# Low parts of the state space mixer's input weights made during the first feed-forward layer and kept in DRAM

## The chip, the cores and the metric

The kernel runs on one core of one Trainium2 chip. The metric is the device time of one execution in microseconds (us); lower is better. The core has TensorE (PE in the rows, with its weight loads as PEld), VectorE (DVE), ScalarE (ACT), GpSimd (POOL) and SyncE (SP). SP and POOL do little but issue DMAs here. Each engine runs its own instructions strictly in order and waits on semaphores for the others.

## The reference

The reference is a chain of two blocks of two layers each. The change concerns the second block alone: a gated linear attention mixer (GLA), a feed-forward layer, a state space mixer (SSD), and a second feed-forward layer. The feed-forward layer and the input side of the mixer, cut to what matters:

```
def sq_relu_mlp(h, w1, w2):                    # D = 1024, w1: D x 4D, w2: 4D x D
    return jnp.square(jax.nn.relu(h @ w1)) @ w2

def ssd_mixer(uc, ul, w_in, conv_w, conv_b, dt_bias, a_log, d_skip, norm_g, w_out, need_ctx):
    def run(h, s_init, need_y):                # h: 256 context or 256 latent tokens
        z, xbc, dt = jnp.split(h @ w_in, [SSD_DI, SSD_DI + SSD_CONV_DIM], axis=-1)
        xbc = jax.nn.silu(dwconv(xbc, conv_w, conv_b))
        xs, bm, cm = jnp.split(xbc, [SSD_DI, SSD_DI + SSD_GN], axis=-1)
        dt = jax.nn.softplus(dt + dt_bias)
        ... chunked scan over 64-token chunks in 8 groups of 4 heads, both directions ...
        return rms_norm_2(y * jax.nn.silu(z), norm_g) @ w_out, (s_f, s_b)
```

All data are fp32. `w_in` of the mixer has 1024 rows; its columns are z (2048), x (2048), B (1024), C (1024) and dt (64).

## The kernel before, in words

A product with weights in fp32 is made of three products of a shorter format: an operand is split into a high part, its cast, and a low part, what the cast left over. For each column block and each of the eight 128-row steps of the contraction (k-steps below) TensorE adds high weight times high input (L1135), high weight times low input (L1136) and low weight times high input (L1137). Inputs are split once. Weights are split each time they are loaded: `wparts` (L1083) loads a stretch with SP, lets ScalarE cast the high piece (L1100, tile `whi`) and lets VectorE subtract it from the loaded weight (L1101, tile `wlo`). `dense_pool(size, bufs)` sets how many columns a piece has and how many pieces can stand ready: 1024 and 4 in the feed-forward layers, 512 and 4 in the mixer. `dense_t` gives transposed outputs, `dense_n` (L1141, products L1155 to L1157) outputs by token rows.

The first feed-forward layer (`ffn(0)`) works on 512 tokens, context and latents. The SSD mixer (`ssd`) first normalizes and modulates its input (`mod_t`), makes dt and its running sums, and then goes over 8 groups. `ssd_in(g)` makes a group's inputs one group ahead: a product "both" of 384 columns (256 of x, 128 of B) for 512 tokens, 72 matmuls of 512 columns, and a product "latents" of 384 columns (128 of C, 256 of z) for 256 tokens, 72 matmuls of 256 columns. Each is followed by a convolution on VectorE (tile `cacc`). `ssd_group(g)` does the scan of the group before: copies of transposed x on ScalarE (`xn`), decays (`dec`, 16 exponents' inputs and 4 exponents), the row `cB` of 2048 columns (ScalarE, then VectorE), and small matmuls (`py`, `tp`). A group's weights come as 5 and 3 k-steps in two DMAs each.

The order on each engine is set at build time by a scheduler that works from a program's dependences, its own estimates of times and priorities: the two split instructions carry a higher priority than what is written around them (`high_priority(offset=300)`). On the chip the orders are fixed. Work that is to run beside other work is written as a generator; `tick` runs it one piece further.

Of the kernel before, what the change touches and what calls it, by code (L numbers as in the profile page):

```python
# [19 lines left out]
P = 128  # L20
# [17 lines left out]
class Kern:  # L38
    def __init__(self, tc, A, ctx):
        self.tc = tc  # L40
        self.nc = tc.nc
        self.A = A
        self.ctx = ctx
        self.cp = ctx.enter_context(tc.tile_pool(name="cp", bufs=1))
        self.cp0 = self.cp
        self.mods, self.beside = {}, None
        self.xp = ctx.enter_context(tc.tile_pool(name="xp", bufs=1))
# [6 lines left out]
        self.wown, self.wlen = None, 2048  # L54
        self.uid = 0
        self.consts()
# [1024 lines left out]
    def wparts(self, wap, k0, kn, cols):  # L1081
# [11 lines left out]
        for k1 in range(0, kn, ks):  # L1093
            hi = self.dp.tile([P, size], F32R, tag="whi", bufs=bufs, name=self.name("whi"))
            lo = self.dp.tile([P, size], F32R, tag="wlo", bufs=bufs, name=self.name("wlo"))
            kk = min(ks, kn - k1)
# [8 lines left out]
    def wbuf(self):  # L1105
# [3 lines left out]
        return self.wp.tile([P, self.wlen], F32, tag="w", bufs=self.wbufs, name=self.name("w"))  # L1109

    def wall(self, wap, nkd, cols):
        n = sum(c[1] for c in cols)
# [3 lines left out]

    def dense_t(self, xh, xl, wap, nkd, cols, emit, n=512, role="mm", parts=1):

# [6 lines left out]
        kw = dict(skip_group_check=True)  # L1125
        ws = self.wall(wap, nkd, cols)
        if parts > 1:
            ws = list(ws)
        for i in range(parts):
            t = slice(i * n // parts, (i + 1) * n // parts)  # L1130
            for k, wh, wl in ws:
                for b in range(nb):
# [3 lines left out]
                    nc.tensor.matmul(a, wh[:, cs], xl[:, k, t], start=False, stop=False, **kw)  # L1136
                    nc.tensor.matmul(a, wl[:, cs], xh[:, k, t], start=False, stop=k == nkd - 1, **kw)  # L1137
        for b in range(nb):
            emit(b, acc[b // pb][:, b % pb])

    def dense_n(self, xs, wap, nkd, cols, emit, mt, role="mm", row0=0, by_tile=False):  # L1141
# [17 lines left out]
        if by_tile:  # L1159
            ws = list(ws)  # L1160
            for m in range(mt):
                for w in ws:
                    step(m, *w)
                emit(m, acc[m][:, 0])
            return
        for w in ws:
            for m in range(mt):
                step(m, *w)
        for m in range(mt):
            emit(m, acc[m // pb][:, m % pb])  # L1170
# [636 lines left out]
    def ssd(self, X, gr, mods, spill):  # L1807
# [4 lines left out]
        self.roles.update(mm=[0, 1, 2, 3, 4], tp=[5, 6], py=[7])  # L1812
        with self.dense_pool(512, 4), self.tc.tile_pool(name=self.name("ssd"), bufs=1, reuse_waits="tile") as gp:
            xh, xl = self.slot(2, [P, KD, 512], F32R), self.slot(3, [P, KD, 512], F32R)
# [30 lines left out]
            self.norm_z(X, 0, *self.factors(st, 0, 2))  # L1845
        return X, gr

    def ssd_in(self, g, xh, xl, W, gp):
# [18 lines left out]

        self.dense_t(xh, xl, W, KD, [(2048 + 256 * g, 256), (4096 + 128 * g, 128)], put)
        self.dense_t(xh[:, :, S:], xl[:, :, S:], W, KD, [(5120 + 128 * g, 128), (256 * g, 256)], put_l, S)
        return xT, bT, cT, zs  # L1870
# [102 lines left out]
    def block2(self, x, mods, out):  # L1973
        X, gr, ctx = self.gla(x)
        self.gk.close()
        gr = self.ffn(0, X, mods[0], (1, 0), 2, 3, gr, ctx=ctx)
        X, gr = self.ssd(X, gr, mods[1], self.drp.tile([S, D], F32, name="x_ssd"))
# [55 lines left out]
```

## Time and profile before

| what | value |
|---|---|
| median of 3 runs | 2223.16 us (2219.62 to 2271.85) |
| the profiled execution's own time | 2227.16 us |
| its span in the profile | 2225.4 us |
| mean granted TensorE clock of that span | 0.962 of full speed |
| TensorE, VectorE, ScalarE busy | 92%, 63%, 40% of the span |
| GpSimd | 3%, 142 instructions |
| DMA | 464.60 MB moved, mean 209 GB/s |

The profile is of one execution on the one core. The busy shares are means over stages with different limits, so the stages are read one by one. By their instructions' lines they lie, from the span's start, at about 1245 to 1300 us (the end of the GLA mixer and the normalization behind it), 1300 to 1642 us (first feed-forward layer), 1642 to 1720 us (the mixer's input and its first products), 1720 to 1950 us (its groups), 1950 to 2003 us (last group and output product). The second feed-forward layer follows.

### The profile page before, as it was taken

Reading aid. Unit: us, or ns where it says so; the run is one execution under the profiler, and the core shown is the slowest. Engines: PE = TensorE matmul, PEld = TensorE weight load, DVE = VectorE, ACT = ScalarE, POOL = GpSimd, SP = SyncE. Lnnn points to the kernel's source line nnn. Section 1 sums busy time; section 2 is a strip of 40 time slices with the busy share of each in tenths; the row PEclk is TensorE's granted clock in tenths of the full one; section 3 lists DMA queues with packets and bytes.
Section 4 is the critical chain, followed back from the end, with each engine's and each line's share of the span. In section 5 each row is a group of like instructions: output and inputs, shape, how many; then the busy total and the mean of one; then the engine's idle time right before and its main releaser. Section 6 shows DMA issues by size and latency. Waiting matters only on the chain. (4 is left out here: it accounts for less than half of the span.)

```text
span 2225.4 us, 34842 instructions
## 1 busy us (share of the span) xinstructions
PE 2053.6 (92%) x13545; PEld 1584.1 (71%) x13545; DVE 1403.1 (63%) x3139; ACT 889.3 (40%) x1788; POOL 62.7 (3%) x142
## 2 busy tenths in 40 slices
PE   8999999896999999988799899999988999997997
PEld 7889655542787855543577598888877888877896
DVE  6864543545776553544786765444476999987666
ACT  5442233211454232221564432322335676755443
POOL 1000000000000000000000000000000000000001
PEclk9997999998999999999999999999998999998998
DMA  8656699888563899898655543223223343445552
GB/s 269 242 189 221 241 329 387 320 320 314 198 242 115 316 326 358 335 362 332 222 211 199 201 141 114 95 95 95 81 70 119 105 134 122 128 168 180 186 193 76
DMA packets 224962, 464.60 MB, mean 209 GB/s; under 512 B 32221, under 2 KB 111741, under 8 KB 217881
## 3 DMA queue, kind: packets, MB, share of 16 engines
q1 hardware_dynamic: 217080, 439.34, 55.8%
q0 software_dynamic: 7712, 22.99, 3.0%
q8 instruction: 108, 1.77, 0.3%
q14 instruction: 62, 0.50, 0.1%
HBM read 457.93 MB, written 4.36 MB: 208 GB/s over the span
## 5 line engine op out<-in xcount | busy, mean ns | idle before, releaser
L1101 DVE TENSOR_TENSOR wlo<-w,whi 128x512 fp32r<-128x512 f32 (+4 forms) x528 | 402.8, 773 | 289.2 <-ACT whi L1100 286.3
L1100 ACT CAST whi<-w 128x512 fp32r<-128x512 f32 (+4 forms) x528 | 358.3, 690 | 546.6 <-PE mm L1136 180.5
L1156 PE MATMUL mm<-wlo,xh 128*128 128x256 f32 (+1 forms) x544 | 159.5, 294 | 0.3 <-DVE wlo L1101 0.2
L1155 PE MATMUL mm<-whi,xh 128*128 128x256 f32 (+1 forms) x544 | 158.9, 294 | 1.0 <-ACT whi L1100 1.0
L1157 PE MATMUL mm<-whi,xl 128*128 128x256 f32 (+1 forms) x544 | 158.1, 292 | 0.0
L1156 PE MATMUL acc<-wlo,hh 128*128 128x512 f32 x384 | 148.6, 389 | 0.0
L1155 PE MATMUL acc<-whi,hh 128*128 128x512 f32 x384 | 147.7, 389 | 0.0
L1157 PE MATMUL acc<-whi,hl 128*128 128x512 f32 x384 | 146.0, 389 | 0.0
L1135 PE MATMUL mm<-s__2932_15020,whi 128*128 128x256 f32 (+1 forms) x384 | 131.0, 346 | 8.2 <-ACT etot L1786 3.9
L1136 PE MATMUL mm<-s__2933_15021,whi 128*128 128x256 f32 (+1 forms) x384 | 129.4, 342 | 0.0
L1137 PE MATMUL mm<-s__2932_15020,wlo 128*128 128x512 f32 (+1 forms) x384 | 118.8, 348 | 3.3 <-DVE wlo L1101 3.3
L1156 PEld LDWEIGHTS mm<-wlo,xh 128*128 128x128 f32 x544 | 105.8, 195 | 11.1 <-DVE isc L407 2.4
L1136 PE MATMUL mm<-s__2108_10494,whi 128*128 128x512 f32 (+1 forms) x320 | 110.3, 348 | 0.5 <-DVE s__2108_10494 L92 0.5
L1155 PEld LDWEIGHTS mm<-whi,xh 128*128 128x128 f32 x544 | 105.7, 195 | 6.3 <-issue 2.7
L1137 PE MATMUL mm<-s__2107_10493,wlo 128*128 128x512 f32 (+1 forms) x320 | 109.1, 350 | 0.9 <-DVE wlo L1101 0.9
L1135 PE MATMUL mm<-s__2107_10493,whi 128*128 128x512 f32 (+1 forms) x320 | 108.3, 349 | 1.1 <-ACT whi L1100 1.1
L1157 PEld LDWEIGHTS mm<-whi,xl 128*128 128x128 f32 x544 | 105.7, 195 | 0.8 <-issue 0.7
L818 PE MATMUL gu<-wx,xg 128*32 128x256 f32 x1024 | 94.2, 390 | 1.7 <-DMA wx<-in_expert_w_up_dram 1.6
L1135 PEld LDWEIGHTS mm<-s__2932_15020,whi 128*128 128x128 f32 x384 | 73.7, 192 | 17.4 <-ACT whi L1100 4.2
L1802 DVE SCALAR_TENSOR_TENSOR cacc<-mm,cvw,cacc 128x508 f32<-128x508 f32 (+3 forms) x128 | 82.2, 672 | 4.3 <-ACT cacc L1798 4.1
L1157 PEld LDWEIGHTS acc<-whi,hl 128*128 128x128 f32 x384 | 72.1, 188 | 15.0
L1156 PEld LDWEIGHTS acc<-wlo,hh 128*128 128x128 f32 x384 | 72.1, 188 | 14.8
(697 smaller groups left out, 4675.8 us busy)
## 6 DMA issues: line engine op xcount, KB each, us to landing
w<-in_ffn_w_dram SPq DMA_DIRECT2D x64, 1024.0 KB, 5.2
wx<-in_expert_w_down_dram SPq DMA_DIRECT2D x38, 1024.0 KB, 10.6
wx<-in_expert_w_up_dram SPq DMA_DIRECT2D x34, 1024.0 KB, 9.2
adaw<-in_ada_w_dram SPq DMA_DIRECT2D x32, 1024.0 KB, 6.6
wx<-in_expert_w_gate_dram SPq DMA_DIRECT2D x32, 1024.0 KB, 6.4
w<-in_expert_w_down_dram SPq DMA_DIRECT2D x28, 1024.0 KB, 11.8
w<-in_expert_w_gate_dram SPq DMA_DIRECT2D x26, 1024.0 KB, 9.9
w<-in_w_in_dram SPq DMA_DIRECT2D x24, 1024.0 KB, 8.8
```

The costliest lines, as they stand in the source:

```text
L818: nc.tensor.matmul(gu[j * CAP:(j + 1) * CAP, c * EH:(c + 1) * EH], xg[:, k, s:s + CAP], w(c, j, k), start=k == 0 and c == 0, stop=k == KD - 1,
L1100: nc.scalar.copy(hv, v[:, k1:k1 + kk])
L1101: nc.vector.tensor_sub(lv, v[:, k1:k1 + kk], hv.bitcast(F32))
L1135: nc.tensor.matmul(a, wh[:, cs], xh[:, k, t], start=k == 0 and b % pb == 0 and i == 0, stop=False, **kw)
L1136: nc.tensor.matmul(a, wh[:, cs], xl[:, k, t], start=False, stop=False, **kw)
L1137: nc.tensor.matmul(a, wl[:, cs], xh[:, k, t], start=False, stop=k == nkd - 1, **kw)
L1155: self.nc.tensor.matmul(a, h[:, sl], wh, start=k == 0 and m % pb == 0, stop=False, **kw)
L1156: self.nc.tensor.matmul(a, h[:, sl], wl, start=False, stop=False, **kw)
L1157: self.nc.tensor.matmul(a, o[:, sl], wh, start=False, stop=k == nkd - 1, **kw)
L1802: nc.vector.scalar_tensor_tensor(acc[:, :, t0:t1], a[:, :, t0 + o:t1 + o], w(t), acc[:, :, t0:t1], op0=OP.mult, op1=OP.add)
```

## The change

During `ffn(0)` a generator `presplit` runs beside the layer, moved on by `step`, which `dense_t` and `dense_n` now call. It has 48 items, one for each 512-column block (12) and each pair of k-steps (4). An item loads 512 KB of `ssd_w_in` with a DMA from POOL into `raw` (two buffers), casts two halves of 128x512 on ScalarE into `hi` (one buffer), subtracts them on VectorE into one half of a ring `parts`, and writes the 512 KB of low parts to DRAM (`lows`) with another DMA from POOL. Its tiles lie in space that GLA's constants had.

In the mixer `ssd_in` takes its weights from `wlows`: high pieces are loaded and cast as before, low pieces come from `lows`, two k-steps at a time, by two DMAs from SP into a `wlo` tile of 768 columns with four buffers. High pieces have three buffers instead of four. The splits of dt's weights and of the output product stay as they were.

```diff
+    def step(self):
+        if self.inner:
+            self.inner += 1
+            if self.inner % 5 in (1, 3):
+                self.tick()
...
+    def wlows(self, wap, nkd, cols, low):
...
+                nc.sync.dma_start(v[:, :, o:o + cn], wap[k0 * P:(k0 + kn) * P, c0:c0 + cn].rearrange("(k p) n -> p k n", p=P))
...
+            for k in range(kn):
+                if (k0 + k) % 2 == 0:
+                    lo = low(k0 + k, 2)
+                hi = self.dp.tile([P, 512], F32R, tag="whi", bufs=self.pieces[1], name=self.name("whi"))[:, :n]
+                with self.tc.high_priority(offset=300):
+                    nc.scalar.copy(hi, v[:, k])
+                yield k0 + k, hi, lo[:, (k0 + k) % 2]
...
-        with self.dense_pool(512, 4), self.tc.tile_pool(name=self.name("ssd"), bufs=1, reuse_waits="tile") as gp:
+        with self.dense_pool(512, 3), self.tc.tile_pool(name=self.name("ssd"), bufs=1, reuse_waits="tile") as gp:
+            self.wlow = 768
...
+    def presplit(self, W, pool, ring):
...
+        todo = [(c, k) for c in (4, 8, 10, 0, 5, 1, 6, 9, 11, 2, 7, 3) for k in range(0, KD, 2)]
...
+                t = raws[n] = pool.tile([P, 2, 512], F32, tag="raw", bufs=2, name=self.name("raw"))
+                nc.gpsimd.dma_start(t, W[k * P:(k + 2) * P, c * 512:c * 512 + 512].rearrange("(k p) n -> p k n", p=P))
...
+        for n, (c, k) in enumerate(todo):
+            load(n + 1)
...
+            for j in range(2):
+                hi = pool.tile([P, 512], F32R, tag="hi", bufs=1, name=self.name("hi"))
+                nc.scalar.copy(hi, raw[:, j])
...
+                nc.vector.tensor_sub(lo[:, :, j], by_g(raw[:, j]), by_g(hi.bitcast(F32)))
+            nc.gpsimd.dma_start(d[:, :, k:k + 2], lo.bitcast(F32))
+            yield
...
+        self.dense_t(xh, xl, W, KD, both, put, ws=parts(both))
+        self.dense_t(xh[:, :, S:], xl[:, :, S:], W, KD, latents, put_l, S, ws=parts(latents))
...
+            self.beside, self.inner = self.presplit(self.A["ssd_w_in_2"][0], pre, ring), 1
+            gr = self.ffn(0, X, mods[0], (1, 0), 2, 3, gr, ctx=ctx)
+            self.tick(100)
```

Three places show how the engines' orders change. The numbers at names are buffers; lines of the changed program are some 10 to 80 higher than before. First VectorE at the start of the mixer, where dt is made (`dt_t`) while the first group's products run. Before:

```order
L1754 RECIPROCAL dt_t_15157<-dt_t_15157 128x256
L1101 TENSOR_TENSOR wlo_15392<-w_15362,whi_15391 128x384
L1755 TENSOR_TENSOR dt_t_15157<-dt_t_15157,dt_t_15156 128x256
L1101 TENSOR_TENSOR wlo_15405<-w_15362,whi_15404 128x384
L1756 TENSOR_TENSOR dt_t_15156<-dt_t_15157 128x256
L1757 TENSOR_SCALAR dt_t_15158<-dt_t_15156 128x256
L1101 TENSOR_TENSOR wlo_15418<-w_15362,whi_15417 128x384
L1759 SCALAR_TENSOR_TENSOR dt_t_15158<-dt_t_15158,dt_t_15156 128x256
L1101 TENSOR_TENSOR wlo_15434<-w_15430,whi_15433 128x384
```

The same place in the changed program:

```order
L1786 RECIPROCAL dt_t_15606<-dt_t_15606 128x256
L1787 TENSOR_TENSOR dt_t_15606<-dt_t_15606,dt_t_15605 128x256
L1788 TENSOR_TENSOR dt_t_15605<-dt_t_15606 128x256
L1789 TENSOR_SCALAR dt_t_15607<-dt_t_15605 128x256
L1791 SCALAR_TENSOR_TENSOR dt_t_15607<-dt_t_15607,dt_t_15605 128x256 x6
L1792 SCALAR_TENSOR_TENSOR dt_t_15607<-dt_t_15607,dt_t_15606 128x256
L1793 TENSOR_SCALAR dt_t_15605<-tp_15600 128x256
L1794 SCALAR_TENSOR_TENSOR dt<-dt_t_15607,dt_t_15605 128x256
L1795 TENSOR_TENSOR dt_t_15608<-dt,tp_15611 128x256
```

The chain of dt now stands in one piece; the ten subtractions that stood in it before (four are shown) are gone.

Second ScalarE a little later, where the first decays and the row cB stand among the casts of the next group's weights. Before:

```order
L1930 ACTIVATE dec_15819<-dec_15819 128x512
L1930 ACTIVATE dec_15826<-dec_15826 128x512
L1933 ACTIVATE cB_15750<-cB_15750 128x2048
L1100 CAST whi_15547<-w_15492 128x384
L1930 ACTIVATE dec_16209<-dec_16209 128x512
L1100 CAST whi_15563<-w_15560 128x384
```

The same place in the changed program:

```order
L1836 ACTIVATE bT_15669<-cacc_15797 128x512
L1969 COPY xn_16185<-tp_16192 128x512
L2012 ACTIVATE dec_16252<-dec_16252 128x512
L1136 CAST whi_15975<-w_15933 128x384
L2010 ACTIVATE dec_16634<-cB_16579,dcum 128x128
L1136 CAST whi_15989<-w_15933 128x384
L2012 ACTIVATE dec_16259<-dec_16259 128x512
L1136 CAST whi_16003<-w_16000 128x384
L2015 ACTIVATE cB_16183<-cB_16183 128x2048
```

`whi_15547` is the piece of the group's fifth k-step, `whi_15975` that of the fourth; the copies `xn` have moved ahead of the cast, the row cB behind three casts.

Third VectorE at the normalization in front of the first feed-forward layer, where the factors of a row are made from its statistics. Before:

```order
L1180 BN_AGGR nz_mv_12369<-ln_st_10497 128x2
L1182 TENSOR_SCALAR nz_v_12372<-nz_mv_12369 128x2
L114 TENSOR_SCALAR rs_t_12375<-nz_v_12372 128x2
L117 TENSOR_SCALAR rs_h_12378<-nz_v_12372 128x2
L115 TENSOR_SCALAR nz_r_12374<-rs_t_12375 128x2
```

The same place in the changed program:

```order
L1909 TENSOR_TENSOR parts<-raw_12749,hi_12836 128x4x128
L1212 BN_AGGR nz_mv_12369<-ln_st_10497 128x2
L1214 TENSOR_SCALAR nz_v_12372<-nz_mv_12369 128x2
L115 TENSOR_SCALAR rs_t_12375<-nz_v_12372 128x2
L118 TENSOR_SCALAR rs_h_12378<-nz_v_12372 128x2
L116 TENSOR_SCALAR nz_r_12374<-rs_t_12375 128x2
L1909 TENSOR_TENSOR parts<-raw_12749,hi_12839 128x4x128
```

Subtractions of two items (`parts`, from `raw`) now stand in this chain, four in all up to the normalization itself (two are shown). Four more stand in the chain that modulates the context's rows at the end of the GLA mixer, 1250 to 1265 us before.

## Rows read from the trace of the kernel before

**Rows 1.** Page: busy time of each engine; the chain that ended last.

```profile
PE 2053.6 (92%) x13545; PEld 1584.1 (71%) x13545; DVE 1403.1 (63%) x3139; ACT 889.3 (40%) x1788; POOL 62.7 (3%) x142
...
PE 19%; DVE 2%; ACT 1%; issue 0%; ACTq 0%; DVEq 0%
```

**Rows 2.** Stretches: busy us (and instructions) of each engine, granted clock, DMA share.

```profile
core 0: us, PE busy (x) PEld busy (x) DVE busy (x) ACT busy (x) POOL busy (x), PEclk, DMA share, GB/s
1250.00:1255.00 5.00, 2.19 (x10) 0.98 (x10) 2.27 (x5) 3.44 (x7) 0.00 (x0) 0.84 1.05 401
...
1340.00:1360.00 20.00, 20.00 (x89) 16.54 (x89) 9.69 (x13) 5.55 (x8) 0.00 (x0) 1.00 0.33 106
1655.00:1720.00 65.00, 55.73 (x282) 45.48 (x281) 45.10 (x86) 36.05 (x79) 2.71 (x4) 0.89 0.34 108
1720.00:1950.00 230.00, 220.66 (x1526) 192.71 (x1525) 216.54 (x420) 155.63 (x346) 6.50 (x10) 1.00 0.41 127
...
1950.00:2003.00 53.00, 49.79 (x309) 40.08 (x308) 44.34 (x102) 26.77 (x55) 0.00 (x0) 0.94 0.45 158
```

**Rows 3.** TensorE's waits, 1720 to 1950 us: us in total, times, longest.

```profile
PE tp L1890 <- ACT xn L1887: 3.8, 3, 1.6
PE mm L1137 <- DVE wlo L1101: 3.3, 5, 1.4
PE mm L1156 <- DVE wlo L1101: 1.0, 1, 1.0
PE tp L1903 <- DVE bn L87: 0.9, 1, 0.9
```

**Rows 4.** TensorE's waits, 1642 to 1720 us.

```profile
PE mm L1135 <- ACT etot L1786: 3.9, 1, 3.9
PE mm L1135 <- ACT whi L1100: 3.4, 1, 3.4
```

**Rows 5.** Groups of lines on VectorE, 1720 to 1950 us: low pieces.

```profile
L1101 DVE TENSOR_TENSOR wlo<-w,whi 128x384 fp32r<-128x384 f32 x104 | 54.9, 548 | 5.9 <-ACT whi L1100 4.4 <-PE mm L1137 1.5
```

**Rows 6.** VectorE's timeline, 1678 to 1691 us: first and last wlo among dt.

```profile
1680.05 0.49 DVE L1101 TENSOR_TENSOR wlo<-w,whi 128x384 fp32r<-128x384 f32 x1
...
1689.98 0.56 DVE L1101 TENSOR_TENSOR wlo<-w,whi 128x384 fp32r<-128x384 f32 x1 [0.18 <-ACT whi L1100]
1690.45 0.41 DVE L1763 TENSOR_TENSOR dt_t<-dt,tp 128x256 f32<-128x256 f32 x1
```

**Rows 7.** TensorE's timeline, 1686 to 1700 us: dt's sums, the next group's first matmul.

```profile
1691.01 0.63 PE L1767 MATMUL tp<-pre,dt_t 128*32 128x128 f32 x8 [1.38 <-DVE dt_t L1763]
...
1698.91 0.77 PE L1135 MATMUL mm<-s__2932_15020,whi 128*128 128x512 f32 x1 [3.86 <-ACT etot L1786]
```

**Rows 8.** ScalarE's timeline, 1700 to 1715 us: first decay, row cB, next cast.

```profile
1701.75 0.40 ACT L1928 ACTIVATE dec<-cB,dcum 128x128 f32<-128x128 f32 x1 [2.92 <-DMA cB<-cum_rows]
...
1711.71 1.90 ACT L1933 ACTIVATE cB<-cB 128x2048 f32<-128x2048 f32 x1
1713.51 0.50 ACT L1100 CAST whi<-w 128x384 fp32r<-128x384 f32 x1
```

**Rows 9.** TensorE's waits, 1240 to 1310 us.

```profile
PE mm L1060 <- DVE scr L1076: 2.8, 1, 2.8
...
PE mm L1060 <- ACT scr L1074: 2.2, 1, 2.2
```

**Rows 10.** Groups of lines, 1245 to 1300 us: pieces of 128x512 on VectorE, ScalarE.

```profile
L1101 DVE TENSOR_TENSOR wlo<-w,whi 128x512 fp32r<-128x512 f32 x16 | 10.8, 686 | 6.9 <-ACT whi L1100 6.8
...
L1100 ACT CAST whi<-w 128x512 fp32r<-128x512 f32 x16 | 9.8, 622 | 11.1 <-PE mm L1157 6.4 <-DVE wlo L1101 3.0 <-DMA w<-in_gla_w_out_dram 1.6
```

**Rows 11.** ScalarE's casts at L1100, 1310 to 1640 us: min/median/max ns, first and last start.

```profile
L1100 ACT CAST whi<-w x58: 1047/1055/1069, 1311.7 to 1620.9; 128x1024 fp32r<-128x1024 f32 x58
```

**Rows 12.** DMA issues, 1280 to 1330 us: KB each, us from issue to landing.

```profile
s__2483_12177<-in_ln_g_dram POOLq DMA_DIRECT2D x1, 512.0 KB, 3.6
s__2483_12177<-in_ln_b_dram POOLq DMA_DIRECT2D x1, 512.0 KB, 6.8
```

**Rows 13.** DMA issues, 1640 to 1960 us.

```profile
w<-in_ssd_w_in_dram SPq DMA_DIRECT2D x15, 384.0 KB, 3.4
...
s__3605_18474<-x_ssd POOLq DMA_DIRECT2D x1, 1024.0 KB, 10.0
```

More of the change, by code (lines that the diff above doesn't have):

```diff
@@ L46, in __init__ @@
         self.mods, self.beside = {}, None
+        self.inner = 0
         self.xp = ctx.enter_context(tc.tile_pool(name="xp", bufs=1))
@@ L53, in __init__ @@
         self.wturn = 0
-        self.wown, self.wlen = None, 2048
+        self.wown, self.wlen, self.wlow = None, 2048, None
         self.uid = 0
@@ L1094, in wparts @@
             hi = self.dp.tile([P, size], F32R, tag="whi", bufs=bufs, name=self.name("whi"))
-            lo = self.dp.tile([P, size], F32R, tag="wlo", bufs=bufs, name=self.name("wlo"))
+            lo = self.dp.tile([P, self.wlow or size], F32R, tag="wlo", bufs=4 if self.wlow else bufs, name=self.name("wlo"))
             kk = min(ks, kn - k1)
@@ L1109, in wbuf @@
         return self.wp.tile([P, self.wlen], F32, tag="w", bufs=self.wbufs, name=self.name("w"))
+    def wlows(self, wap, nkd, cols, low):
+        nc = self.nc
+        n = sum(c[1] for c in cols)
+        kl = self.wlen // n
+        for k0 in range(0, nkd, kl):
+            kn = min(kl, nkd - k0)
+            v = self.wbuf()[:, :kn * n].rearrange("p (k n) -> p k n", k=kn)
+            o = 0
+            for c0, cn in cols:
+                nc.sync.dma_start(v[:, :, o:o + cn], wap[k0 * P:(k0 + kn) * P, c0:c0 + cn].rearrange("(k p) n -> p k n", p=P))
+                o += cn
+            for k in range(kn):
[5 more added lines that the diff above has]
+                yield k0 + k, hi, lo[:, (k0 + k) % 2]
     def wall(self, wap, nkd, cols):
@@ L1125, in dense_t @@
         kw = dict(skip_group_check=True)
-        ws = self.wall(wap, nkd, cols)
+        ws = ws or self.wall(wap, nkd, cols)
         if parts > 1:
@@ L1163, in dense_n @@
                     step(m, *w)
+                    if m % 2:
+                        self.step()
                 emit(m, acc[m][:, 0])
@@ L1168, in dense_n @@
                 step(m, *w)
+            self.step()
         for m in range(mt):
@@ L1866, in put_l, with parts @@
                 nc.vector.scalar_tensor_tensor(zs[:, b - 1], zs[:, b - 1], 1.0, a, op0=OP.add, op1=OP.mult)
-        self.dense_t(xh, xl, W, KD, [(2048 + 256 * g, 256), (4096 + 128 * g, 128)], put)
-        self.dense_t(xh[:, :, S:], xl[:, :, S:], W, KD, [(5120 + 128 * g, 128), (256 * g, 256)], put_l, S)
+        def parts(cols):
+            low = [(c0 // 512, c0 % 512 // n) for c0, n in cols]
+            return self.wlows(W, KD, cols, lambda k, kn: self.low(low, k, kn))
+        both, latents = [(2048 + 256 * g, 256), (4096 + 128 * g, 128)], [(5120 + 128 * g, 128), (256 * g, 256)]
+        self.dense_t(xh, xl, W, KD, both, put, ws=parts(both))
+        self.dense_t(xh[:, :, S:], xl[:, :, S:], W, KD, latents, put_l, S, ws=parts(latents))
         return xT, bT, cT, zs
@@ L1975, in block2 @@
         self.gk.close()
-        gr = self.ffn(0, X, mods[0], (1, 0), 2, 3, gr, ctx=ctx)
+        with self.tc.tile_pool(name="pre", bufs=1, side="right") as pre:
+            ring = self.xp.tile([P, 2, D], F32R, tag="x", bufs=1, name="parts")
+            self.beside, self.inner = self.presplit(self.A["ssd_w_in_2"][0], pre, ring), 1
+            gr = self.ffn(0, X, mods[0], (1, 0), 2, 3, gr, ctx=ctx)
+            self.tick(100)
+            self.beside, self.inner = None, 0
         X, gr = self.ssd(X, gr, mods[1], self.drp.tile([S, D], F32, name="x_ssd"))
```

26 lines of the change are left out of this document (25 added, 1 removed).

## The prediction

> **What bounds the kernel now.** I read the page's chain first: TensorE carries 19% of the span in the chain that ended last, VectorE 2%, ScalarE 1%, so VectorE's 63% of busy time says little until it is split by stage [rows 1]. The second view is the stretches [rows 2]. In the first feed-forward layer, where the new work is put, TensorE is busy 20.00 of 20 us at full clock while VectorE uses 9.69 and ScalarE 5.55: a pure TensorE stage with idle splitters. In the mixer's groups, where work is taken away, VectorE is busy 216.54 of 230 us, yet TensorE is busy 220.66: of 230 us only 9.3 are not already matmul time. The start of the mixer (1655 to 1720 us) leaves 65 - 55.73 = 9.3 us, its tail (1950 to 2003) 53 - 49.79 = 3.2 us. The third view is what TensorE waited for in these holes: in the groups 4.3 us for low pieces, 0.9 us for another VectorE instruction, 3.8 us for ScalarE's copies of x [rows 3]; at the start 3.9 us for ScalarE's etot and 3.4 us for a high piece [rows 4]. So the most that the whole mixer could give back as idle time is 9.3 + 9.3 + 3.2 = 21.8 us, 1% of the run, and less than half of it names VectorE.
>
> **The change part by part.** The sum is made against the profiled execution, 2227.16 us, 4.0 us above the median of 2223.16; at the end I take those 4 us off again.
>
> The splits in the groups. The change removes 16 subtractions per group, 128 in all; 104 of them took 54.9 us between 1720 and 1950 us [rows 5], which leaves VectorE at 216.5 - 54.9 = 161.6 of 230 us. That is 54.9 us off an engine that waits or is waited for, but TensorE gets back only the holes that name it: 3.3 + 1.0 + 0.9 = 5.2 us [rows 3]. The 3.8 us for xn stay: ScalarE casts as many high pieces as before. Gain 5.2 us, with bounds of 0 (ScalarE comes last in the same places) and 9.3 (all holes close).
>
> High pieces with three buffers. A piece "both" feeds nine matmuls of 512 columns; 89 of them in 20.00 us [rows 2] make 0.225 us each, so a piece lasts 2.0 us. ScalarE can thus leave the casts for 6 us instead of 8 before TensorE runs dry. No row shows a queue of three. The nearest is the start's burst: from the first decay at 1701.75 to the next cast at 1713.51 are 11.8 us, after which TensorE had waited 3.4 us with four pieces [rows 8, 4]. In the groups the four waits listed make 9.0 of the 9.3 us and none is for a high piece [rows 3], so four pieces were ample there; I take 1.5 us for all seven groups, near to nothing, with bounds of 0 (less lead gains nothing) and one piece, 2.0 us, in each, 14.
>
> The start of the mixer. Ten subtractions stand among dt's instructions on VectorE, from 1680.05 to 1690.45 us [rows 6]. Without them 10 x 0.49 to 0.56, about 5 us, leave the chain. But TensorE was at work until 1689.6 and waited only 1.38 us for dt [rows 7], so of the 5 us at most 1.4 come back there. The changed order also puts dt's sums nine matmuls of 256 columns ahead of the end of "latents", 9 x 0.112 = 1.0 us by half of 0.225. The way from there to the next group, 1691.01 to 1698.91 us through ScalarE and VectorE [rows 7], starts 1.4 + 1.0 = 2.4 us earlier. Then comes the burst: the order has the cast of the fourth piece where that of the fifth was, with the copies xn ahead of it and the row cB of 1.90 us behind it [rows 8]. It comes about as much earlier as it is longer, and is needed one piece, 2.0 us, earlier, so the 3.4 us grow by some 1.7. Net gain 0.7 us. Bounds: 7.3 (both waits of rows 4 go), and a loss of 2.
>
> The tail. Group 7 and the output product, whose splits stay, leave 3.2 us idle [rows 2]; a VectorE without backlog may give back a third: gain 1, bounds 0 and 3.2.
>
> New loads in the mixer. SP issues 24 DMAs per group instead of 8, of 256 and 128 KB; the nearest row is 384 KB landing in 3.4 us [rows 13], with 41% of the DMA engines in use [rows 2]. Four buffers of two pieces are eight k-steps ahead, over 8 us even in "latents" (8 x 9 x 0.112). Cost nothing; the cover is that lead, and a landing over 8 us would cost its excess per tile. The first group's tiles have only to wait for the first layer's space, and mod_t lies between.
>
> The items in the first layer. 48 items are 96 casts of 0.62 and 96 subtractions of 0.69 us [rows 10]: 60 us on ScalarE and 66 on VectorE, in some 320 us in which these have 14 and 10 of every 20 us free [rows 2]. What can go wrong is order, not load: ScalarE casts this layer's weights every (1620.9 - 1311.7) / 57 = 5.42 us [rows 11], the order puts about one item in each interval, and a cast that waits for an item's load holds up the weights behind it. A buffer of `raw` goes round in 0.53 us of issue, the landing L and some 2.6 us of casts and subtractions (two of each); with two buffers an item takes (L + 3.1) / 2. With the nearest rows, POOL's 512 KB in 3.6 and 6.8 us [rows 12], that is 3.4 to 5.0 us, inside 5.42. Cost nothing; TensorE's matmuls are the cover, with four pieces, 4 x 5.42 = 21.7 us, in hand.
>
> The items before the layer. They start at the end of the GLA mixer, where TensorE is no cover: it was busy 2.19 of 5 us and the DMA engines fully (1.05 at 401 GB/s) [rows 2], and it waited 2.8 us for VectorE and 2.2 us for ScalarE in the chain that modulates the context [rows 9]. The first two loads are 1 MB, 2.6 us of that bandwidth, beside the load of the output weights: I take half, 1.3. Four subtractions and four casts stand in the chain, 4 x (0.69 + 0.62) = 5.2 us, of which two engines side by side show less than half: 2. Four more subtractions stand in the factors of the next normalization, 4 x 0.6 = 2.4 us; that chain had little slack, since TensorE waits behind it: 2. Together 5.3 us, with bounds of 0 (all beside other work; nothing is removed there that could gain) and 11 (all in series and a load late by 1 to 2 us).
>
> Sum: -5.2 + 1.5 - 0.7 - 1 + 5.3 = -0.1 us. The profiled execution would take 2227, a median execution 2223 us. The gain is real but as small as the idle time that TensorE had, and the cost in the place with no cover eats it.
>
> **The rivals.**
> *More comes back.* All holes that the mixer has go except ScalarE's 3.8 us: 21.8 - 3.8 = 18, and at the start, where the granted clock averaged 0.89 [rows 2], up to 0.11 x 65 = 7 us lost to stretches at 1.2 instead of 2.4 GHz with them; the items cost nothing net. That is 2223 - 25 = 2198 us. For it: VectorE is full for whole stretches and everything queues behind it. Against it: two of the largest waits name ScalarE [rows 3, 4].
> *ScalarE takes the place of VectorE.* Three high pieces don't cover the bursts: 2 us in each of seven groups, 14 us on my sum: 2237 us. For it: the burst of 11.8 us [rows 8]. Against it: ScalarE is busy 155.63 of 230 us [rows 2].
> *The items hold up the first layer* (slower). The mechanism is the one above: a late load, then ScalarE in order, then the weights' casts, then TensorE. It decides at L = 2 x 5.42 - 3.1 = 7.7 us. With the largest landing that POOL has in the mixer, 10.0 us for 1 MB [rows 13], an item takes 6.6 us, and 48 x (6.6 - 5.42) - 21.7 = 35 us are lost: 2258 us. The rows of 512 KB speak against it, but they were measured with one or two POOL loads under way, not with a load and a store at all times.
> The Trainium skill has a rule on this side: "SBUF — State Buffer", section "SBUF: two separate sides", says that DMAs issued from GpSimd can be starved of descriptors while VectorE runs certain one-input instructions, about 620 ns growing to 3100. By it a landing of 6.8 us could become 9.3, an item 6.2 us, and the loss 48 x 0.78 - 21.7 = 16 us, 2239 us. The trace so far shows 3.6 us beside a busy VectorE [rows 12], which speaks against it.
> *The change doesn't do what it says.* The low pieces arrive late at each group, and TensorE waits for DMAs where it waited for VectorE: the 5.2 us stay, and some 10 come on top: 2238 us.
>
> **How the numbers follow.** Chances: forecast 0.55, more comes back 0.15, ScalarE 0.12, the first layer held up 0.13, late pieces 0.05. The forecast's own bounds are about 2208 to 2236. Down to 2198 and up to 2248 the range takes in the rivals on both sides but the far part of the held-up layer and what lies beyond full recovery, some 0.15. A change under 2%, 44 us, can't be told from none here: below 2179 no sum of the idle times leads (0.03), above 2268 only a first layer in which loads take over 10 us (0.05).
>
> **What would show it.** In the new trace: VectorE near 162 of 230 us in the groups and no wait for a low piece but for DMA; TensorE still at 96% or more there; 20 of 20 us busy in the first layer with VectorE near 13 and ScalarE near 9; the layer's own casts 5.4 us apart; more idle time of TensorE at 1250 to 1305 us, by about 5. Wrong would be: gaps in TensorE's work between 1340 and 1620 us behind ScalarE's casts from `raw`; waits for high pieces in every group; or a mixer shorter by 15 us or more.

## The result, and the profile after

The change makes the kernel slower by half a percent: the ratio of the changed kernel's times to those of the kernel before is 1.0056, with a 95% interval of 1.0030 to 1.0083. On the median of 2230.46 us that 17 runs of the kernel before gave, that is 12.5 us (7 to 19). The prediction had no change. The profiled execution took 2250.44 us, 23 us more than the one before; the next table shows that 12.8 of these 23 us lie ahead of GLA's output, where VectorE, ScalarE and GpSimd run the same instructions in the same order as before. The profiled executions of three experiments below (the items alone, no traffic, no low loads) ran at a lower mean granted clock (0.937 to 0.945) and took longer than the others of their kernels, so of them a stretch is compared only where its own clock is like that of the other runs.

The table is made from the start times of matmuls in the trace: the first product of GLA's output, the last of it (L1155, tile `mm`), the first and the last product of the first feed-forward layer, the last product of the mixer's output, and the end of the last matmul.

```
us                                                     before   after
start of the program to first product of GLA's output  1203.9  1216.7
GLA's output, first to last product                      79.2    83.1
gap to the layer                                          2.4     2.4
first feed-forward layer, first to last product         356.3   366.4
mixer: to the last product of its output                370.4   368.2
rest                                                    197.7   197.3
from the first product of GLA's output on              1006.0  1017.5
```

The last row differs by 11.5 us, near the measured difference of 12.5; the first row is that execution's own, not the change. So three numbers are to be explained: 3.9 us at the end of the GLA mixer, 10.1 in the layer, -2.2 in the mixer. Each is from one execution of either kernel. The layer's number repeats: the run with the items alone below has the same order of instructions there on TensorE, VectorE and ScalarE, and its layer took 368.6 us against 366.4. The mixer's does not: in the eight runs below and here that have this mixer, with three high pieces and low loads, it took 368.2 to 371.9 us, 370.1 on average, against 370.4 in the one profile of the kernel before, and the changed kernel's is the shortest of the eight.

The stretches of the profile after (columns as in [rows 2]): three from the layer's first half, one from its second, then the mixer's start, groups and tail.

```profile
1362.00:1382.00 20.00, 17.89 (x74) 14.42 (x74) 11.70 (x16) 7.71 (x11) 5.53 (x8) 0.94 0.85 282
1382.00:1402.00 20.00, 20.00 (x87) 16.45 (x87) 12.48 (x17) 7.10 (x10) 5.32 (x8) 0.97 0.72 245
1462.00:1482.00 20.00, 16.46 (x66) 13.16 (x65) 12.43 (x18) 7.15 (x11) 5.10 (x8) 0.91 0.81 262
1522.00:1542.00 20.00, 20.00 (x90) 16.57 (x89) 14.02 (x19) 11.22 (x18) 5.50 (x8) 1.00 0.79 276
1680.00:1745.00 65.00, 52.99 (x281) 43.31 (x281) 37.42 (x68) 36.22 (x79) 2.71 (x4) 0.92 0.58 174
1745.00:1975.00 230.00, 222.36 (x1528) 192.48 (x1528) 168.05 (x313) 154.77 (x344) 5.21 (x8) 1.00 0.69 210
1975.00:2028.00 53.00, 48.61 (x309) 37.86 (x308) 46.42 (x105) 27.68 (x57) 1.35 (x3) 1.00 0.46 154
```

Where the layer had 20.00 us of work in 20 [rows 2], two stretches now have 17.89 and 16.46 at a mean clock of 0.94 and 0.91: TensorE stops, and part of what follows runs at 1.2 instead of 2.4 GHz. The whole layer, before and after:

```profile
1285.50:1641.80 356.30, 354.55 (x1742) 301.19 (x1743) 180.21 (x280) 109.09 (x144) 2.03 (x4) 1.00 0.30 96
1302.20:1668.60 366.40, 358.56 (x1741) 303.39 (x1742) 234.12 (x366) 157.11 (x230) 60.86 (x88) 0.99 0.64 220
```

TensorE's idle time rose from 356.30 - 354.55 = 1.8 us to 366.40 - 358.56 = 7.8, by 6.1 us. Three stretches of the layer beyond its start, at 0.94, 0.97 and 0.91 of full clock, lose about (0.06 + 0.03 + 0.09) x 20 = 3.6 us. Idle time and lost clock together make 9.7 of the 10.1 us. In the groups VectorE fell from 216.54 to 168.05 us, by 48.5 of the 54.9 forecast, and TensorE gained less than 2 us of 230 by it. The waits of TensorE name the holes; in the layer (1302 to 1672 us) the first line is new, the second was there before:

```profile
PE acc L1184 <- DVE scr L1262: 5.6, 2, 3.5
PE mm L1163 <- ACT whi L1108: 1.1, 1, 1.1
```

At the start of the mixer (1672 to 1745 us) two waits stand where [rows 4] had 3.9 and 3.4. In the groups (1745 to 1975 us) the waits for low pieces and for xn [rows 3] are gone, and others, for high pieces above all, stand in their place:

```profile
PE tp L1972 <- DVE bT L1837: 7.7, 1, 7.7
PE mm L1163 <- DVE cacc L1834: 3.0, 1, 3.0
```

```profile
PE mm L1163 <- ACT whi L1136: 4.4, 8, 0.9
PE tp L1985 <- ACT bn L86: 1.5, 1, 1.5
PE tp L1985 <- DVE bn L88: 1.3, 1, 1.3
```

How the layer's wait of 3.5 us comes about is read from three timelines of the same 10 us. TensorE first: its next product needs an accumulator that VectorE has yet to empty (L1262).

```profile
1471.76 0.69 PE L1184 MATMUL acc<-whi,hh 128*128 128x512 f32 x1 [3.54 <-DVE scr L1262]
```

Ahead of that evacuation VectorE has the items' subtractions (`parts`), which wait for a cast:

```profile
1463.10 0.69 DVE L1909 TENSOR_TENSOR parts<-raw,hi 128x512 fp32r<-128x512 f32 x1 [2.04 <-ACT hi L1907]
...
1468.24 0.69 DVE L1909 TENSOR_TENSOR parts<-raw,hi 128x512 fp32r<-128x512 f32 x1 [3.06 <-ACT hi L1907]
...
1470.93 1.28 DVE L1262 TENSOR_TENSOR scr<-acc,s__2483_12177 128x512 f32<-128x512 f32 x2
```

And ScalarE's casts wait for the items' loads:

```profile
1462.45 0.62 ACT L1907 CAST hi<-raw 128x512 fp32r<-128x512 f32 x1 [2.64 <-DMA raw<-in_ssd_w_in_dram]
...
1467.59 0.62 ACT L1907 CAST hi<-raw 128x512 fp32r<-128x512 f32 x1 [3.13 <-DMA raw<-in_ssd_w_in_dram]
```

The DMA issues of 1345 to 1600 us show how long these take (KB each, us to landing), against 3.6 and 6.8 us for the two of this size that [rows 12] had:

```profile
w<-in_ffn_w_dram SPq DMA_DIRECT2D x23, 1024.0 KB, 5.5
lows<-parts POOLq DMA_DIRECT2D x37, 512.0 KB, 5.1
raw<-in_ssd_w_in_dram POOLq DMA_DIRECT2D x35, 512.0 KB, 6.4
```

The layer's own casts are not what TensorE waits for: their four pieces of lead held. At the mixer's start ScalarE waits for the rows of running sums to make their way through DRAM (before, its first decay waited 2.92 us for the row cB [rows 8]), and the convolutions that TensorE needs stand behind it:

```profile
1721.30 0.78 ACT L1830 ACTIVATE cacc<-mm,cvb,cvw 128x512 f32<-128x512 f32 x1 [2.24 <-DMA cum_rows<-dt_t]
...
1728.86 4.78 ACT L2010 ACTIVATE dec<-cB,dcum 128x128 f32<-128x128 f32 x16 [4.62 <-DMA cB<-cum_rows]
```

From dt's sums on TensorE (1691.01 us before [rows 7], 1713.7 after) to the first decay (1701.75 [rows 8], 1728.86) these are 10.7 and 15.2 us. The DMA issues say where nearly all of these 4.5 us went: the store of the running sums, 64 KB, which the row cB has to wait for, took 1.9 us to land before (first line) and 6.2 after (second).

```profile
cum_rows<-dt_t POOLq DMA_DIRECT2D x1, 64.0 KB, 1.9
cum_rows<-dt_t POOLq DMA_DIRECT2D x1, 64.0 KB, 6.2
```

### The profile page after: what moved, and what is told of

It is laid out like the page before. It is cut to its first block, busy times and chain, and to the rows that moved or that the text cites. A ratio compares the mean times of both kernels' runs of the same rounds, so it can differ in the third digit from the quotient of the medians.

```text
span 2248.4 us, 35244 instructions
## 1 busy us (share of the span) xinstructions
PE 2067.3 (92%) x13545; PEld 1592.1 (71%) x13545; DVE 1406.4 (63%) x3107; ACT 942.9 (42%) x1884; POOL 130.2 (6%) x238
## 5 line engine op out<-in xcount | busy, mean ns | idle before, releaser
L1109 DVE TENSOR_TENSOR wlo<-w,whi 128x512 fp32r<-128x512 f32 (+3 forms) x400 | 335.4, 845 | 195.0 <-ACT whi L1108 193.9
L1108 ACT CAST whi<-w 128x512 fp32r<-128x512 f32 (+3 forms) x400 | 294.4, 746 | 366.1 <-PE mm L1186 127.0
L1163 PE MATMUL mm<-s__3088_15469,whi 128*128 128x512 f32 (+1 forms) x384 | 137.4, 358 | 9.1 <-ACT whi L1136 4.4
L1165 PE MATMUL mm<-s__3088_15469,wlo 128*128 128x512 f32 (+1 forms) x384 | 130.6, 340 | 0.0
L1164 PE MATMUL mm<-s__3089_15470,whi 128*128 128x512 f32 (+1 forms) x384 | 130.3, 339 | 0.0
L1164 PE MATMUL mm<-s__2108_10494,whi 128*128 128x512 f32 (+1 forms) x320 | 110.5, 349 | 0.9 <-DVE s__2108_10494 L93 0.9
L1165 PE MATMUL mm<-s__2107_10493,wlo 128*128 128x512 f32 (+1 forms) x320 | 109.4, 350 | 0.9 <-DVE wlo L1109 0.9
L1163 PE MATMUL mm<-s__2107_10493,whi 128*128 128x512 f32 (+1 forms) x320 | 107.7, 350 | 1.1 <-ACT whi L1108 1.1
L1909 DVE TENSOR_TENSOR parts<-raw,hi 128x512 fp32r<-128x512 f32 x96 | 66.1, 688 | 54.3 <-ACT hi L1907 53.8
L1907 ACT CAST hi<-raw 128x512 fp32r<-128x512 f32 x96 | 59.4, 619 | 95.9 <-DMA raw<-in_ssd_w_in_dram 59.3
L1136 ACT CAST whi<-w 128x384 fp32r<-128x384 f32 x128 | 64.4, 512 | 69.7 <-PE mm L1164 62.8
```

The source lines that it names most:

```text
L1108: nc.scalar.copy(hv, v[:, k1:k1 + kk])
L1109: nc.vector.tensor_sub(lv, v[:, k1:k1 + kk], hv.bitcast(F32))
L1136: nc.scalar.copy(hi, v[:, k])
L1163: nc.tensor.matmul(a, wh[:, cs], xh[:, k, t], start=k == 0 and b % pb == 0 and i == 0, stop=False, **kw)
L1909: nc.vector.tensor_sub(lo[:, :, j], by_g(raw[:, j]), by_g(hi.bitcast(F32)))
```

## The experiments

Theory A was that the items cost the time, through DMAs that land late and engines that stand in order behind them, and that the mixer's part gains some 2 us. Theory B, the rival, was that the items are covered and the mixer loses, through three high pieces and the extra loads. The ratios are to the kernel before, on the same chip; the stage lengths are those of the table above (GLA's output, layer, mixer) in the run's profile.

**The items alone.** The mixer splits its weights as before:

```diff
-        with self.dense_pool(512, 3), ...
-            self.wlow = 768
+        with self.dense_pool(512, 4), ...
...
-        self.dense_t(xh, xl, W, KD, both, put, ws=parts(both))
+        self.dense_t(xh, xl, W, KD, both, put)
```

> The 48 items are made and stored during the first feed-forward layer, but nothing reads the stored low parts: the mixer splits its weights as before, with four buffers each. Theory A (the items cost the time: loads from POOL land late, ScalarE and VectorE stand in order behind them, TensorE waits for them in the layer and at the end of the GLA mixer; the mixer's own part gains about 2 us): 13 us slower than the kernel before, with VectorE's late evacuation of the accumulators (scr) as TensorE's wait in the layer. Theory B (the items are covered, and the mixer loses through its three high pieces and its extra loads): within 3 us of the kernel before.

Measured: ratio 1.0053 (1.0012 to 1.0095), GLA's output 84.5 us, layer 368.6, and TensorE's wait for `scr` in the layer 6.9 us. The items alone cost what the whole change costs, within the intervals. B fails.

**The low loads alone.** Eight items, started late, and all groups read two column blocks:

```diff
-        todo = [(c, k) for c in (4, 8, 10, 0, 5, 1, 6, 9, 11, 2, 7, 3) for k in range(0, KD, 2)]
+        todo = [(c, k) for c in (4, 8) for k in range(0, KD, 2)]
...
-            d = self.lows[c]
+            d = self.lows[4 if c < 8 else 8]
```

> Leaves out 40 of the 48 items; all groups read the low parts of two column blocks, so their DMAs are as many and as large as in the changed kernel but the data are not each group's own. The eight items start only after the layer's first output block. Theory A: 2 to 4 us faster than the kernel before, which is all that the mixer gets back. Theory B: about as slow as the changed kernel, 10 us or more slower than before. My prediction's own sum for this part was 5 us faster.

Measured: ratio 0.9991 (0.9955 to 1.0026), mixer 369.7 us against 370.4 before. A mixer's part of 1 us or less lies inside the spread of the eight mixers above (368.2 to 371.9); it is less than either sum had. Even the eight items cost the layer 4 us (360.7), in one wait of 4.0 us for `scr`.

**The items late.** The first load waits for the layer's first output block, through a copy of one column:

```diff
+                if n < gate:
+                    nc.vector.tensor_copy(t[:, 0, :1], src[:, :1])
                 nc.gpsimd.dma_start(t, W[k * P:(k + 2) * P, c * 512:c * 512 + 512].rearrange("(k p) n -> p k n", p=P))
```

> The changed kernel, but the first item's load waits for the layer's first output block, so that no item runs at the end of the GLA mixer or in the normalization in front of the layer. Theory A: these 4 us come back, but the items have 70 us less and run to the layer's end, so TensorE still waits in the layer, 9 to 15 us: 7 to 13 us slower than the kernel before. If the cost in the layer were only that of the crowded start, it would be gone: within 2 us of the kernel before. Theory B: as slow as the changed kernel.

Measured: ratio 1.0060 (1.0015 to 1.0105); GLA's output 78.7 us (the 4 us are back), layer 374.8: the waits for `scr` are now three of 9.1 us in all. The layer's cost is not that of the crowded start. Over all runs GLA's output took 80.3 us on average in the seven with the late start (78.7 to 82.1) and 83.6 in the six others with items (82.4 to 84.6), so the part of the cost that lies there is 3.3 us.

**Half the load.** Both casts and both subtractions of an item work on the one k-step that is loaded.

```diff
-                nc.gpsimd.dma_start(t, W[k * P:(k + 2) * P, c * 512:c * 512 + 512].rearrange("(k p) n -> p k n", p=P))
+                nc.gpsimd.dma_start(t[:, :1], W[k * P:(k + 1) * P, c * 512:c * 512 + 512].rearrange("(k p) n -> p k n", p=P))
```

> Each item loads only one of its two k-steps (256 KB instead of 512) and splits it twice, so casts, subtractions, stores and the mixer are as in the changed kernel, with 12.6 MB of loads less; the low parts of every second k-step are those of its neighbour. Theory A with the load as the cause: an item takes some 4 instead of 6 us, the waits in the layer go, and 2 to 4 us of loss at the end of the GLA mixer stay against 2 of gain: 0 to 3 us slower than the kernel before. If the casts and subtractions themselves are the cause: as slow as the changed kernel, 10 us or more.

Measured: ratio 1.0057 (1.0012 to 1.0102), which is the number of the expectation's second branch; the stages tell a different story. The layer fell to 359.6 us and TensorE's wait for `scr` there is gone. But GLA's output took 84.6 us and the gap behind it 5.0 instead of 2.4: in front of the layer ScalarE's casts of items waited 5.0 us for loads (0.7 in the changed kernel, with as many of them there). Why the smaller loads came later there is not settled. The landing in 1300 to 1600 us barely fell with the bytes:

```profile
raw<-in_ssd_w_in_dram POOLq DMA_DIRECT2D x42, 256.0 KB, 5.8
```

**Three load buffers**, then the same with the late start. The high part is cast into the ring, which frees the tile `hi`:

```diff
-                t = raws[n] = pool.tile([P, 2, 512], F32, tag="raw", bufs=2, name=self.name("raw"))
+                t = raws[n] = pool.tile([P, 2, 512], F32, tag="raw", bufs=3, name=self.name("raw"))
...
-                nc.scalar.copy(hi, raw[:, j])
+                nc.scalar.copy(lo[:, :, j], by_g(raw[:, j]))
```

> The changed kernel with three buffers for an item's load instead of two, and the high part cast into the ring itself (so that no single buffer ties ScalarE to VectorE's last subtraction); one low-part buffer of the layer's hidden tiles is given up for the space. Theory A with the load's latency as the cause: an item takes (6.4 + 3) / 3 = 3 us, the waits in the layer go, and the layer, 356.3 us before from first to last product and 366.4 in the changed kernel, takes 357 to 360; in all 2 to 5 us slower than before. If the bulk of casts, subtractions and bytes is the cause: the layer stays at 364 or more.

> As the run with three load buffers, and the first loads also wait for the layer's first output block. Theory A: the end of the GLA mixer is as before (79 us), the layer 357 to 362 us, the mixer part 2 us shorter: within 3 us of the kernel before, the best that this change can be. If the order of items alone matters and not their loads: the layer takes as long as with the late start alone, 374 us.

Measured: ratios 1.0030 (0.9990 to 1.0070) and 1.0012 (0.9967 to 1.0058); layer 361.2 and 360.6 us, GLA's output 84.4 and 79.9. Half of the layer's 10 us came back, not all. The waits of ScalarE in the first of the two runs (1260 to 1620 us) show what is late next: the store of the ring's half, no longer the load.

```profile
ACT parts L1908 <- DMA lows<-parts: 67.9, 37, 4.6
```

**No traffic.** This separates the instructions from their DMAs. From the ninth item on nothing is loaded or stored; casts and subtractions stay. All groups read the low parts of two column blocks.

```diff
-            if n < len(todo):
+            if n < 8:
...
-            nc.gpsimd.dma_start(d[:, :, k:k + 2], lo.bitcast(F32))
+            if n < 8:
+                nc.gpsimd.dma_start(d[:, :, k:k + 2], lo.bitcast(F32))
```

> The changed kernel with the loads and stores of the first 8 items alone; the other 40 items cast and subtract what stands in the two load buffers and store nothing, and all groups read the low parts of two column blocks. All 96 casts and 96 subtractions are in the layer, 80 of them without a DMA to wait for. If the wait is for DMAs that take 5 to 7 us with two buffers each: the layer takes 356 to 358 us as before (366.4 in the changed kernel), and the whole 1 to 5 us more than the kernel before, from the end of the GLA mixer. If the instructions themselves, in order on ScalarE and VectorE, are the cause: the layer takes 362 us or more.

Measured: ratio 0.9992 (0.9945 to 1.0038), layer 356.9 us. TensorE is at 20.00 of 20 us beside VectorE at up to 15.29 (a stretch of the layer's first half):

```profile
1500.00:1520.00 20.00, 20.00 (x90) 16.56 (x89) 15.29 (x22) 9.50 (x13) 0.00 (x0) 1.00 0.32 106
```

With all 192 instructions at work the layer, at full clock throughout, takes 0.6 us more than before. The scheduler also put them at other places in this run, so order is a rival; the traces decide against it. Of the layer's 32 evacuations (L1262) 4 stand directly behind a subtraction in the changed kernel and 12 in this run, yet here TensorE waits for none of them. What is gone are VectorE's long waits for the items' casts (first line the changed kernel, second this run; us in total, times, longest):

```profile
DVE parts L1909 <- ACT hi L1907: 53.8, 36, 3.4
DVE parts L1909 <- ACT hi L1907: 21.2, 30, 1.3
```

What cost 10 us were the waits for the DMAs' round trips. The ratio shows no cost, where the expectation had 1 to 5 us from the end of the GLA mixer (82.7 us here); the interval allows it.

**Loads by SP.** One word is changed, `nc.gpsimd` to `nc.sync` at the load.

> The changed kernel with the items' loads issued by SP instead of POOL, the stores still by POOL. A load of half the bytes had landed in 5.8 instead of 6.4 us, so bytes are not what it waits for. If the load waits behind the store in POOL's queue, or for POOL to write its descriptors (the theory that the prediction's page rule speaks for): landings of 3.5 to 5 us and the layer 357 to 361 us instead of 366.4. If the 16 DMA engines are simply shared: landings of 6 us or more and the layer 364 us or more. The end of the GLA mixer stays at 83 us in both.

Measured: ratio 1.0133 (1.0053 to 1.0212), layer 379.1 us. The landing in 1300 to 1600 us is as long as from POOL:

```profile
raw<-in_ssd_w_in_dram SPq DMA_DIRECT2D x39, 512.0 KB, 6.5
```

The load's landing does not hang on POOL as its issuer, so the starved descriptors of GpSimd's DMAs that the Trainium skill describes ("SBUF — State Buffer", "SBUF: two separate sides") are not what these traces show. And SP has loads of its own behind: it waited 109.5 us for an item's subtraction to free a buffer, and TensorE 16.7 us in two waits for ScalarE's relu.

**The mixer with four high pieces**, on top of the run with the low loads alone:

```diff
-        with self.dense_pool(512, 3), ...
+        with self.dense_pool(512, 4), ...
...
-        t = self.dp.tile([P, 768], F32R, tag="wlo", bufs=4, name=self.name("wlo"))
+        t = self.dp.tile([P, 768], F32R, tag="wlo", bufs=3, name=self.name("wlo"))
```

> The run with the low loads alone (eight items only), with four buffers for high pieces and three for low tiles instead of three and four. If three high pieces are too few: the 5.6 us of waits for high pieces in the groups go, and the mixer takes 364 to 366 us instead of 369.6. If ScalarE's order is the limit whatever the buffers: 368 to 371 us.

Measured: ratio 1.0015 (0.9970 to 1.0061), mixer 365.9 us, 3.8 less than in the run with the low loads alone and 4.5 less than before. The four runs with four pieces have the same order of instructions in the mixer and took 364.6 to 369.2 us there, 366.5 on average, 3.6 less than the eight with three. In 1720 to 1950 us TensorE is busy 225.87 us, and its wait for high pieces is down from 5.6 us in the run with the low loads alone to 1.1:

```profile
1720.00:1950.00 230.00, 225.87 (x1551) 197.58 (x1550) 175.97 (x328) 157.23 (x352) 6.54 (x10) 1.00 0.71 222
```

```profile
PE mm L1163 <- ACT whi L1136: 1.1, 2, 1.0
```

**No low loads.** One tile, filled once, is every low part; no items; the output has no meaning.

```diff
+            self.clow = gp.tile([P, 768], F32R, name="clow")
+            nc.vector.tensor_copy(self.clow, X[:, 0, :768])
```

> No items, and no loads of low parts: all products of the mixer's input take one tile, filled once, as the low part, so the mixer does neither the subtractions nor the loads. The mixer (last product of the layer to last of the output product) took 370.4 us before, 368.2 in the changed kernel and 369.6 with the low loads alone. If the low loads' traffic (a later row cB at the start) eats the gain: 362 to 365 us, and the wait at the start falls from 7 to 10 us to 3 to 4. If ScalarE and three high pieces are what is left: 368 to 370 us.

Measured: ratio 0.9955 (0.9922 to 0.9989), 10 us faster (2 to 17). The layer (356.3 us), GLA's output (80.2) and the rest (197.1) are as before, so this gain is the mixer's: it would take some 360 us (353 to 368), which favours the first expectation over the second, if not by much. The profile doesn't show the gain: its mixer took 375 us, in an execution of 2274.09 us against this kernel's median of 2227.17, and decides nothing between the two.

The waits say more. The store of the running sums landed as early as before, after 2.2 us:

```profile
cum_rows<-dt_t POOLq DMA_DIRECT2D x1, 64.0 KB, 2.2
```

With the items alone, where the mixer also has no low loads, it took 1.9 us; in the eight runs with low loads and three high pieces it took 4.6 to 6.2, in those with four 3.1 to 3.9. So the low loads delay the row cB. ScalarE waited 1.20 and 3.24 us for the two DMAs where it waited 2.24 and 4.62 in the changed kernel:

```profile
1734.97 0.78 ACT L1830 ACTIVATE cacc<-mm,cvb,cvw 128x512 f32<-128x512 f32 x1 [1.20 <-DMA cum_rows<-dt_t]
...
1742.45 2.16 ACT L2004 ACTIVATE dec<-cB,dcum 128x128 f32<-128x128 f32 x7 [3.24 <-DMA cB<-cum_rows]
```

But TensorE's waits at the start hardly shrank: 7.7 us for bT became 1.8 for xT, while a high piece is now waited for, and with the convolution it is 9.8 us instead of 10.7. The expected fall to 3 to 4 us did not come.

```profile
PE mm L1163 <- ACT whi L1136: 4.3, 1, 4.3
PE mm L1163 <- DVE cacc L1834: 3.7, 1, 3.7
```

The high pieces' waits in the groups stayed too (5.7 us). Both causes are there; how many us of the mixer each takes is not settled by this run.

**Mended versions.** Late start, three load buffers with the tile `hi` kept, four high pieces; loads by SP with late start and four high pieces; and the run with three load buffers and the late start, with four high pieces.

> All mends together: first loads wait for the layer's first output block, three load buffers with the separate high tile kept (eleven of the layer's hidden tiles instead of twelve make the space), and in the mixer four high pieces with three low tiles. Theory A: end of the GLA mixer 79 us as before, layer 357 to 361 us (356.3 before), mixer 366 us (370.4 before): between 5 us faster and 1 us slower than the kernel before. If the ring's stores bind the items as they did when the high part was cast into the ring: layer 361 us or more, 0 to 3 us slower.

> Loads by SP, the first ones only after the layer's first output block, two load buffers, and four high pieces with three low tiles in the mixer. If SP's loads land earlier: layer 357 to 362 us instead of the 374.8 with the late start alone, mixer 366 us, end of the GLA mixer 79 us: 5 us faster to 1 us slower than the kernel before. If not: layer 370 us or more, 8 us or more slower.

> The run with three load buffers, the high part cast into the ring and the late start (layer 360.8 us, end of the GLA mixer 79.9), with the four high pieces and three low tiles in the mixer that gave 364.5 us there. Sum of the stages: 0.7 + 4.6 - 5.9 = 0.6 us faster than the kernel before; between 4 us faster and 4 us slower. If the mixer's gain does not hold beside another layer: 4 to 6 us slower.

Measured: ratios 1.0066 (1.0023 to 1.0108), 1.0136 (1.0068 to 1.0205) and 0.9999 (0.9959 to 1.0039). The first has the shortest mixer (364.6 us) and a layer of 374.2, a miss of my expectation: with three load buffers ScalarE waits for a load 9.1 us in all, but for VectorE's subtractions, and these for the ring's store.

```profile
ACT hi L1912 <- DVE parts L1914: 95.0, 63, 6.1
...
ACT hi L1912 <- DMA raw<-in_ssd_w_in_dram: 9.1, 5, 2.5
```

```profile
DVE parts L1914 <- DMA lows<-parts: 45.6, 21, 5.6
```

The second has the faults of loads by SP (layer 386.9 us). The third gives the kernel before's time to within the interval: layer 360.0 us, 3.7 above before, mixer 369.2, 1.2 below. Its mixer did not keep the 365 to 366 us of the others. The order there is the same as in the other runs with four pieces, so this is a spread between executions: TensorE was idle for 24.8 us against 21.6 to 24.2, at a mean clock of 0.95 against 0.96. No run here beats the kernel before while it makes the low parts itself.

## Why the prediction was wrong

**The step that failed** is "The items in the first layer ... Cost nothing". The forecast worked with 3.6 to 6.8 us per load and an item of 3.4 to 5.0 us against 5.42 available, and watched the layer's weights as the thing that would be held up. Measured are a landing of 6.4 us, and 5.1 for the store, which the sum left out of the ring altogether. A landing of 6.4 us is still under the 7.7 at which the prediction's rule would lose time, so the rule itself missed the cost: the average period does not decide. ScalarE and VectorE run in order, and the order fixed at build time put evacuations (`scr`) behind subtractions that wait. Waits in line of 2 to 3.4 us reach TensorE there, with no lead of 21.7 us in between, and the clock, which fell behind both of these stops, adds more than half as much again: 6.1 us of idle time and some 3.6 of lost clock make 9.7 of the 10.1. The rival that named "the items hold up the first layer" had the right place and sign, the wrong victim (the layer's weights instead of its evacuations) and the wrong price: 10.1 us, not 35. The run without traffic shows that the waits for the DMAs' round trips are the cause; the run with half the bytes and that with SP's queue show that neither the bytes alone nor the load's queue is, and a third load buffer brings back half.

**The end of the GLA mixer**: forecast 5.3 us, measured 3.9 in the profile and 3.3 over the runs with and without a late start. The size is right within the stated bounds, the make-up only in part: of the 2 us forecast for the next normalization, which lies in the layer's first 40 us, there is next to nothing (TensorE idle 2.2 us there before, 2.4 after).

**The splits in the groups**: 5.2 us forecast as the holes that name VectorE. The 4.3 us for low pieces did close, and the 3.8 for xn, forecast to stay, with them; the wait for bn did not (1.3 us). TensorE's idle time of 9.3 us became 7.6, since 4.4 us for high pieces and 1.5 for ScalarE's bn came in. **Three high pieces** were taken as 1.5 us; the runs with four pieces give 3.6 to 3.8. The size was off, by a factor of about two and a half; the argument for the small value, that four pieces showed no wait, said nothing about three.

**The start of the mixer**: 0.7 us gain forecast; the waits there became 10.7 us instead of 7.3, since the row cB came 4.5 us later after dt's sums. "New loads in the mixer ... Cost nothing" looked at the loads' own lead and not at what else uses the DMA engines: their share rose from 0.34 to 0.58 at the start and from 0.41 to 0.69 in the groups [rows 2]. That the low loads delay cB is shown by the store of its sums, 1.9 to 2.2 us without them and 4.6 to 6.2 with them beside three high pieces. How much of TensorE's wait goes back to it is open, since without the low loads a wait for a high piece took its place.

**The mixer in sum**: -5.4 us forecast, -2.2 in the profile and -0.3 on average over the eight runs with this mixer, which is none to within their spread. With -0.1 forecast for all and +11.5 found in the profile, the layer's 10.1 us are most of the error; the mixer's missing gain adds 3.2, and the end of the GLA mixer, cheaper than forecast, takes off 1.4. VectorE in the groups (161.6 forecast, 168.05) came near, and no wait for low pieces came as written.

## What to carry to other kernels

Work moved under a stage whose engine is full is not free because the engines that do it have idle time: here a cast that waited 3 us for a DMA delayed everything behind it on two engines that run in order. Before calling such work covered, look for what those engines must deliver promptly (here an accumulator's evacuation), and ask of every buffer in the moved chain whether it covers the round trip. A third load buffer brought back half of the layer's cost here, and then the stores were late; no run gave the stores more depth. A stage with little idle time on the bounding engine gives back only that idle time; a buffer given up to pay for the move (here one high piece, some 3.6 us) can take most of it. And a stage's length in one profile carries its own spread: the same mixer took 364.6 to 369.2 us in four of them, as much as the gain looked for.

## What the runs showed of the hardware that was not expected

A DMA of 256 KB landed in 5.8 us where one of 512 KB took 6.4, and 512 KB took 6.5 us from SP as against 6.4 from POOL: beside this steady stream the landing hardly followed the bytes or the issuing engine. A store of 64 KB took 1.9 us to land before, and 6.2 beside the low loads. A single wait of TensorE of 3.5 us lies in a stretch of 20 us with a mean clock of 0.91, by which 1.8 us more were lost. And up to GLA's output, with the same order on VectorE and ScalarE, twelve of the fifteen profiled executions took 1189.9 to 1219.6 us and the other three up to 1249.4. The twelve alone spread over more than twice the change's effect, which is why the stages were compared from there on.
